# Weights, states and small tables of a one-core decoder layer, laid out by the host in reading order

## The chip, the cores and the metric

The kernel runs on one core of a Trainium2 chip. The metric is device time in microseconds (us) of one execution, given as the median of several runs. TensorE (PE) does the matrix products, VectorE (DVE) and ScalarE (ACT) the element-wise work. SyncE (SP) and GpSimd (POOL) issue the transfers (DMAs) between the chip's memory (HBM) and the on-chip buffers, SP nearly all of the loads and POOL most of the stores. All of them share 16 DMA engines.

## The reference: what is computed

One layer of a hybrid decoder, run for a prompt of 512 tokens and for 8 sampled sequences of 8 tokens, 576 tokens in all, in float32:

```python
h = rms_norm(x, norm_pre_mix)
proj = jnp.einsum('btd,de->bte', h, w_in)              # 1024 -> 8208
qkv, z, a, b, uv, gates = jnp.split(proj, SPLIT_POINTS, axis=-1)
o_a, new_buf, s_new = delta_branch(qkv, z, a, b, conv_buf, s0, ...)
o_b, v_rows = chunk_mlp_branch(uv, sgu_ln_w, sgu_ln_b, w_spatial, b_spatial)
merged = (sigmoid(g_a) * (o_a @ w_proj_a) + sigmoid(g_b) * (o_b @ w_proj_b))
x = x + rms_norm(merged @ w_out, norm_post_mix)
gate, up = jnp.split(rms_norm(x, norm_pre_ffn) @ w_ffn_in, 2, axis=-1)
x = x + rms_norm((silu(gate) * up) @ w_ffn_out, norm_post_ffn)
```

`delta_branch` is a causal convolution of width 4 over q, k and v and then a gated delta rule in chunks, which inverts a triangular matrix for each chunk and head. `chunk_mlp_branch` mixes the tokens of a chunk with a lower triangular 128 x 128 matrix for each of 8 channel groups.

## The kernel before

Activations lie with the features on the 128 partitions. A product of 1024 input features with 128 output columns is one unit: its weights are loaded as a tile `wraw` of 128 partitions x 8 x 128 floats (512 KB), ACT rounds them to a tile `whi`, DVE subtracts to get the rest `wlo`, and PE runs three products, whi with the rounded activations, wlo with the rounded activations, and whi with the rest of the activations (L255 to L307, the products at L282, a split of any other tile at L124 and L310). `wraw`, `whi` and `wlo` have two buffers each, so a load starts when the unit two before it has been split.

The program runs in stages on one in-order instruction stream for each engine: norm of x and its transposition (L192 to L252), the products u and v of the MLP branch with the chunk mixing (L313 to L562), the products with w_proj_b (L564), the delta branch in two groups of 4 heads each (L574 to L1114), the products with w_proj_a, then w_out and the norms, the FFN-in in 22 pairs (L1305), the FFN-out (L1580). In the delta branch `elim` inverts 32 x 32 blocks by a loop of small DVE instructions. It gets its input over memory (`d<-at`, `ae<-d`) and sends its result back over memory (`d<-xe`, then `XH<-d` and `XT<-d`, L796 to L812), on which the products of `combine` (L817 and on) depend. The units of the w_in products fill PE meanwhile, at fixed steps (table FILL).

A scheduler that simulates the program decides the order of each stream at build time. SP issues its DMAs in that order, and one that has to wait holds up all that follow it.

w_in is one array of 1024 rows of 8208 floats. A unit takes 128 columns of it, so a partition gets eight pieces of 512 bytes, from rows 128 apart:

```python
ld(out=raw[:, :nk], in_=w[k0 * P:(k0 + nk) * P, col:col + P].rearrange("(k p) m -> p k m", p=P))
```

w_proj_a, w_proj_b and w_ffn_in are read in the same way from rows of 1024 and 5632 floats. w_ffn_out is read in pieces of 2 KB (L1566), w_out in one run of 4 KB for each partition (L1153). Three kinds of small tables are transposed on PE after loading: the taps of the convolution (`feat`, L250), w_spatial (`wsn`, L448, and for the sampled tokens `wbn` to `wbe`, L453), and the convolution state (`scn`, whose memory has the tag `ae`, L587).

Of the kernel before, what the change touches and what calls it, by code (L numbers as in the profile page):

```python
# [28 lines left out]
CONSTS = ["ident", "mneg", "mneg_s", "seqm4", "ones", "triu", "triu_s", "ones_s", "tril_s", "seqm"]  # L29
# [3 lines left out]
def _host_consts():  # L33
# [15 lines left out]
        "tril_s": ups.T,  # L49
# [43 lines left out]
def _build(ctx, tc, I, O):  # L93
# [5 lines left out]
    w_in = I["w_in"][0]  # L99
# [1547 lines left out]
```

## Time and profile before

| | |
|---|---|
| median of 3 runs | 1226.68 us (1223.93 to 1229.81) |
| the profiled execution | 1224.94 us, of which its span is 1222.8 us |
| mean granted TensorE clock | 0.969 |
| PE busy | 1150.5 us (94%) |
| DVE, ACT, POOL busy | 717.4, 569.9, 149.7 us |
| read from HBM, written | 106.35 MB, 17.06 MB |

The span runs from the first to the last instruction. Busy is the time in which an engine worked on an instruction. PE is idle for 72 us in all. A granted clock of 1.00 is 2.4 GHz and 0.50 is 1.2 GHz; a stretch between them has had both.

### The profile page before, as it was taken

To read this page: it belongs to the slowest core of one execution; us is meant where nothing else is said; L and a number is where in the kernel's file an instruction comes from. 1 tells how busy PE (TensorE), PEld (TensorE's weight loads), DVE (VectorE), ACT (ScalarE), POOL (GpSimd) and SP (SyncE) were. 2 spreads that over 40 slices of the span, in tenths; PEclk is the share of its full clock that TensorE was granted. 3 is DMA by queue.
4 is the path that set the end of the run, shared out by engine and by line. 5 is a ranking of instruction groups with operands and counts; after the bars stand their busy time and mean duration, and the time that the engine had idled before them with its cause. 6 is when DMAs were issued, how large, how long until landed. Compare 5 with 4: busy or idle time off the path is not lost.

```text
span 1222.8 us, 20426 instructions
## 1 busy us (share of the span) xinstructions
PE 1150.5 (94%) x8144; PEld 1075.6 (88%) x8144; DVE 717.4 (59%) x1386; ACT 569.9 (47%) x1227; POOL 149.7 (12%) x230
## 2 busy tenths in 40 slices
PE   6999999999997999999998998969999999899997
PEld 5999999998996998988997886858999999888885
DVE  4329722557873456767554664667777787661323
ACT  5423323884544773558445443435445445441221
POOL 3001210002000021020010100150111111160001
PEclk9999999999997998998999999988999999999999
DMA  6911344443344354654252744023233333212222
GB/s 163 220 59 37 85 127 112 76 88 110 91 110 94 80 132 91 171 131 89 67 137 72 260 136 138 2 68 87 87 93 92 93 104 103 87 53 86 86 87 78
DMA packets 163011, 124.74 MB, mean 102 GB/s; under 512 B 14096, under 2 KB 145713, under 8 KB 162916
## 3 DMA queue, kind: packets, MB, share of 16 engines
q1 hardware_dynamic: 156226, 103.72, 32.8%
q0 software_dynamic: 6544, 19.64, 4.9%
q8 instruction: 64, 1.05, 0.3%
q14 instruction: 31, 0.25, 0.1%
q10 hardware_dynamic: 146, 0.07, 0.0%
HBM read 106.35 MB, written 17.06 MB: 101 GB/s over the span
## 4 chain that ended last, share of the span: by engine, by line
PE 52%; DMA 7%; DVE 5%; ACT 4%; issue 2%; POOL 0%; POOLq 0%; DVEq 0%; ACTq 0%; SPq 0%
PE mmps L282 13%; PE bank L1305 10%; PE mmps L1305 7%; PE bank L1580 6%; PE mmps L1580 6%; DMA wraw<-w_in 2%; PE bank L1198 2%; PE mmps L1198 1%; DVE wlo L124 1%; DMA wraw<-w_out 1%; ACT whi L256 1%; DMA wraw<-w_proj_a 1%; DMA wraw<-w_ffn_out 1%; PE bank L880 1%; DMA XH<-d 1%
## 5 line engine op out<-in xcount | busy, mean ns | idle before, releaser
L282 PE MATMUL mmps<-xh,whi 128*128 128x256 f32 (+1 forms) x896 | 273.3, 305 | 4.8 <-ACT ev L136 2.9
L282 PE MATMUL mmps<-xh,wlo 128*128 128x256 f32 (+1 forms) x896 | 271.8, 304 | 4.5 <-DVE wlo L124 4.5
L282 PE MATMUL mmps<-xl,whi 128*128 128x256 f32 (+1 forms) x896 | 271.8, 304 | 0.0
L124 DVE TENSOR_TENSOR wlo<-wraw,whi 128x1024 fp32r<-128x1024 f32 x114 | 146.6, 1287 | 208.9 <-ACT whi L256 208.7
L256 ACT CAST whi<-wraw 128x1024 fp32r<-128x1024 f32 x114 | 119.3, 1047 | 209.4 <-PE mmps L282 60.2
L282 PEld LDWEIGHTS mmps<-xh,whi 128*128 128x128 f32 x896 | 174.3, 195 | 7.5 <-ACT ev L136 4.1
L282 PEld LDWEIGHTS mmps<-xh,wlo 128*128 128x128 f32 x896 | 174.4, 195 | 6.3 <-DVE wlo L124 5.6
L282 PEld LDWEIGHTS mmps<-xl,whi 128*128 128x128 f32 x896 | 174.3, 195 | 0.7 <-issue 0.3
L127 DVE SCALAR_TENSOR_TENSOR ev<-ev,fcol 128x600 f32<-128x600 f32 x72 | 60.1, 837 | 1.8 <-ACT ev L136 0.6
L136 ACT ACT_TABLE_LOAD x40 | 51.3, 1283 | 7.6 <-DVE ans L124 3.2
L1305 PE MATMUL bank<-mh,w2hi 128*128 128x288 f32 x156 | 48.0, 308 | 5.3 <-ACT w2hi L256 5.2
L1305 PE MATMUL bank<-mh,w2lo 128*128 128x288 f32 x156 | 47.5, 305 | 2.3 <-DVE w2lo L124 2.3
L136 ACT ACTIVATE ev<-mmps 128x320 f32<-128x320 f32 (+1 forms) x73 | 30.8, 431 | 38.0 <-PE mmps L282 26.4
L1305 PE MATMUL bank<-ml,w2hi 128*128 128x288 f32 x156 | 47.3, 303 | 0.0
L1283 POOL TENSOR_TENSOR wup<-wraw,wup 128x512 f32<-128x512 f32 x20 | 26.2, 1308 | 172.5 <-DVE wup L1283 150.6
L136 ACT ACTIVATE jk<-bank 128x128 bf16<-128x128 f32 (+1 forms) x112 | 31.2, 279 | 17.6 <-PE bank L952 11.6
L282 PE MATMUL mmps<-obl,whi 128*128 128x320 f32 (+1 forms) x128 | 38.6, 303 | 0.0
L282 PE MATMUL mmps<-obh,wlo 128*128 128x320 f32 (+1 forms) x128 | 38.4, 303 | 0.0
L282 PE MATMUL mmps<-oal,whi 128*128 128x320 f32 (+1 forms) x128 | 37.5, 295 | 0.8 <-DVE oal L124 0.8
L282 PE MATMUL mmps<-oah,wlo 128*128 128x320 f32 (+1 forms) x128 | 37.6, 297 | 0.7 <-DVE wlo L124 0.7
L282 PE MATMUL mmps<-oah,whi 128*128 128x320 f32 (+1 forms) x128 | 37.1, 298 | 0.7 <-ACT oah L310 0.7
L282 PE MATMUL mmps<-obh,whi 128*128 128x320 f32 (+1 forms) x128 | 37.6, 303 | 0.0
(501 smaller groups left out, 2996.3 us busy)
## 6 DMA issues: line engine op xcount, KB each, us to landing
wraw<-w_in SPq DMA_DIRECT2D x56, 512.0 KB, 8.2
wup<-w_ffn_in SPq DMA_DIRECT2D x22, 512.0 KB, 4.6
wraw<-w_ffn_out SPq DMA_DIRECT2D x22, 512.0 KB, 3.7
wraw<-w_ffn_in SPq DMA_DIRECT2D x20, 512.0 KB, 4.0
pgd<-ev POOLq DMA_DIRECT2D x16, 288.0 KB, 5.3
ev<-pgd SPq DMA_DIRECT2D x16, 288.0 KB, 7.8
wraw<-w_proj_b SPq DMA_DIRECT2D x8, 512.0 KB, 4.5
Si<-state_delta SPq DMA_DIRECT2D x16, 256.0 KB, 4.9
```

Of the source, the lines that this page charges most:

```text
L124: return V.tensor_tensor(out=out, in0=a, in1=b, op=op)
L127: V.scalar_tensor_tensor(out=out, in0=a, scalar=s, in1=b, op0=op0, op1=op1)
L136: return S.activation(out=out, in_=a, func=f, scale=scale, accum_out=accum)
L256: a = S.copy(out=hi, in_=raw)
L282: TE.matmul(ps, lhsT=a[:, j, :], rhs=b[k][:, HF[hf]], start=(k == 0 and i == 0), stop=(k == nk - 1 and i == 2))
L880: TE.matmul(px[js, i * P:(i + 1) * P], lhsT=ZT[:, j * 160 + 32 * s:j * 160 + 32 * s + 32], rhs=Si[i, j % 2][:, s], start=(s == 0), stop=(s ...
L1198: TE.matmul(ps[q], lhsT=a[k] if t == 0 else a[k][:, o:o + P], rhs=b[k][:, q * 512:(q + 1) * 512], start=(k == 0 and i == 0), stop=(k == KT ...
L1283: (G if g else V).tensor_tensor(out=out, in0=a, in1=b, op=op)
L1305: TE.matmul(ps, lhsT=w[x][:, j], rhs=b[y][:, j], start=(first and j == 0 and i == 0), stop=(j == KH - 1 and i == 2), skip_group_check=not ...
L1580: TE.matmul(ps, lhsT=x[k] if t == 0 else x[k][:, o:o + P], rhs=unit[w][:, a_], start=(k == 0 and i == 0), stop=(k == FT - 1 and i == len(t ...
```

## The change

The host hands over other arrays. Each unit of w_in, w_proj_a, w_proj_b and w_ffn_in is one block of 128 partitions x 4 KB, in the order in which it is read, and each pair of w_ffn_out as well. The three column blocks of v, with the 16 columns of a and b behind the last, are arrays of their own (`w_v0` to `w_v2`). The states of the delta rule lie as 128 partitions x 2 KB (`state_delta_t`). The taps, w_spatial and the convolution state are transposed by the host, so the 41 transposes on PE with their copies go, and DVE multiplies w_spatial by its mask in place. Eight small loads on POOL (`wbn`) become one on SP, three loads of the convolution state on POOL become one, and the table `tril_s` is dropped from the constants. The bytes that are loaded stay the same but for that and the repeated 8 x 8 blocks. Its core:

```diff
-    w_in = I["w_in"][0]
+    def w_in(col):
+        return I["w_in_t"][col // P if col < C_AB else 32 + (col - C_U) // P if col < C_VM else 40 + (col - C_GA) // P]
...
-    feat = p0.tile([P, P], F32, name="feat", bufs=1)
-    ld(out=feat[0:96], in_=I["conv_w"][0].rearrange("t (n f) -> (t n) f", f=P))
-    ld(out=feat[96:97], in_=I["delta_norm_w"])
+    ld(out=fcol, in_=I["conv_t"])
     xh, xl = cols(XH_), cols(XL_)
-    ps = bank()
-    TE.transpose(ps[:, 0:97], feat[0:97], ident[0:97, 0:97])
-    S.copy(out=fcol, in_=ps[:, 0:97])
...
-        ld(out=raw[:, :nk], in_=w[k0 * P:(k0 + nk) * P, col:col + P].rearrange("(k p) m -> p k m", p=P))
+        ld(out=raw.rearrange("p k m -> p (k m)"), in_=w(col))
...
-            last["v"] = ld(out=raw[:, k0:k0 + 4, :e - c0],
-               in_=w_in[rows, C_VM + c0:C_VM + e].rearrange("(k p) m -> p k m", p=P))
-            if c1 > D:
-                ld(out=raw[:, k0:k0 + 4, e - c0:w], in_=w_in[rows, C_AB:C_AB + 16].rearrange("(k p) m -> p k m", p=P))
+            last["v"] = ld(out=raw[:, k0:k0 + 4].rearrange("p k m -> p (k m)"), in_=I[f"w_v{i}"][:, k0 * w:(k0 + 4) * w])
...
-        ld(out=wsn, in_=I["w_spatial"][0].rearrange("g i j -> i g j"))
+        ld(out=wst, in_=I["w_spatial_t"])
+        ld(out=wbn, in_=I["w_spatial_s"])
...
-    for s in range(8):
-        st(out=wbn[s * 8:(s + 1) * 8], in_=I["w_spatial"][0, :, 0:8, 0:8].rearrange("g i j -> i g j"))
-    wbe = wv.tile([NS, 8, NS], F32, name="wbe")
     with tc.issue_after(last["split"][1].ins):
         for g in range(8):
-            tt(wbe[:, g].rearrange("p (s j) -> p s j", j=8), wbn[:, g].unsqueeze(1).broadcast_to([NS, 8, 8]),
-               c("tril_s").rearrange("p (s j) -> p s j", j=8), ALU.mult)
-    for q in range(2):
-        ps = bank()
-        for j in range(4):
-            TE.transpose(ps[:, j * P:(j + 1) * P], wsn[:, 4 * q + j], ident)
-        tt(wst[:, 4 * q:4 * q + 4], ps.rearrange("p (a b) -> p a b", b=P),
-           c("triu").unsqueeze(1).broadcast_to([P, 4, P]), ALU.mult)
-    ps = bank()
-    for g in range(8):
-        TE.transpose(ps[:NS, g * NS:(g + 1) * NS], wbe[:, g], ident[:NS, :NS])
-    V.tensor_copy(wbt, ps[:NS].rearrange("p (a b) -> p a b", b=NS))
+            tt(wbt[:, g].rearrange("p (s i) -> p s i", i=8), wbn[:, g].unsqueeze(1).broadcast_to([NS, 8, 8]),
+               c("triu_s").rearrange("p (s i) -> p s i", i=8), ALU.mult)
+        for q in range(2):
+            tt(wst[:, 4 * q:4 * q + 4], wst[:, 4 * q:4 * q + 4], c("triu").unsqueeze(1).broadcast_to([P, 4, P]), ALU.mult)
...
-    for q in range(3):
-        scn = dt_([24, D], "ae", 1)
-        st(out=scn, in_=I["state_conv"][0].rearrange("s r f -> (s r) f")[:, q * D:(q + 1) * D])
-        ps = bank()
-        for j in range(8):
-            TE.transpose(ps[:, j * 24:(j + 1) * 24], scn[:, j * P:(j + 1) * P], ident[:24, :24])
-        V.tensor_copy(sct[:, q * 8:(q + 1) * 8, 3:], ps[:, 0:192].rearrange("p (a b) -> p a b", b=24))
+    scn = dt_([P, 24, 24], "ae", 1)
+    st(out=scn, in_=I["state_conv_t"])
+    V.tensor_copy(sct[:, :, 3:], scn)
...
-                    ld(out=Si[i, z], in_=I["state_delta"][0, 4 * z:4 * z + 4, h0 + hh].rearrange("s k v -> k s v"))
+                    ld(out=Si[i, z], in_=I["state_delta_t"][h0 + hh, z])
...
-        ld(out=raw, in_=wfi[:, col:col + P].rearrange("(k p) m -> p k m", p=P))
+        ld(out=raw.rearrange("p k m -> p (k m)"), in_=I["w_ffn_in_t"][col // P])
...
-        ld(out=raw, in_=src)
+        ld(out=raw.rearrange("p a c -> p (a c)"), in_=I["w_ffn_out_t"][q, u])
...
+    def tiles(a):
+        return a.reshape(KT, P, -1, P).transpose(2, 1, 0, 3).reshape(-1, P, KT * P)
+
+    w, out = first("w_in"), {}
+    out["w_in_t"] = tiles(np.concatenate([w[:, :C_AB], w[:, C_U:C_VM], w[:, C_GA:]], axis=1))
```

The order of the streams moves at a few places only. These are SP's rows at the start of the program, behind the five loads of x, first of before and then of the changed kernel (`dtb` holds two small vectors of the gates, `con` constants):

```order
L246 DMA feat<-conv_w 96x128
L247 DMA feat<-delta_norm_w 1x128
L261 DMA wraw<-w_in 128x8x128 x2
L466 DMA dtb<-dt_bias 128x8
L467 DMA dtb<-a_log 128x8
L261 DMA wraw<-w_in 128x8x128 x2
L358 DMA vraw<-w_in 128x4x346 x2
```

```order
L254 DMA fcol<-conv_t 128x97
L265 DMA wraw<-w_in_t 128x1024 x2
L453 DMA dtb<-dt_bias 128x8
L454 DMA dtb<-a_log 128x8
L265 DMA wraw<-w_in_t 128x1024 x2
L359 DMA vraw<-w_v 128x1384 x2
```

One small DMA ahead of the first weights is gone, and each load of weights is one run for each partition.

On PE, in the stage of w_proj_b, the first eight transposes of the convolution state stand between two units (`obh` and `obl` are the two parts of the mixed activations, `ae` the loaded state). Of before:

```order
L282 MATMUL mmps<-obh_1431,whi 128x320
L282 MATMUL mmps<-obh_1431,whi 128x256
L282 MATMUL mmps<-obh_1431,whi 128x320
L587 MATMUL bank<-ident,ae 128x24 x8
L282 MATMUL mmps<-obl_1432,whi 128x320
L282 MATMUL mmps<-obh_1431,wlo 128x320
```

And of the changed kernel:

```order
L286 MATMUL mmps<-obh_1395,whi 128x320
L286 MATMUL mmps<-obh_1395,whi 128x256
L286 MATMUL mmps<-obh_1395,whi 128x320
L286 MATMUL mmps<-obl_1396,whi 128x320
L286 MATMUL mmps<-obh_1395,wlo 128x320
```

The transposes are gone there, and nothing takes their place on PE; the other 16 of them stand in the same stage and go likewise. On DVE the copies of the state become one, which waits for the load instead of for PE. Of before and of the changed kernel:

```order
L783 MEMSET xe 72x1024
L124 TENSOR_TENSOR obl_1432<-ev,obh_1431 128x576
L124 TENSOR_TENSOR obl_1447<-ev,obh_1446 128x576
L784 MEMSET xe 72x32
L588 COPY sct<-bank 128x8x24
L124 TENSOR_TENSOR wlo<-wraw,whi 128x1024
```

```order
L766 MEMSET xe 72x1024
L133 TENSOR_TENSOR obl_1396<-ev,obh_1395 128x576
L133 TENSOR_TENSOR obl_1411<-ev,obh_1410 128x576
L767 MEMSET xe 72x32
L571 COPY sct<-ae 128x24x24
L133 TENSOR_TENSOR wlo<-wraw,whi 128x1024 x7
```

It stands at the same place, ahead of the splits of the w_proj_b units.

## Rows read from the trace of the kernel before

**Rows 1.** The page: busy us, share of the span and instructions of each engine.
```profile
PE 1150.5 (94%) x8144; PEld 1075.6 (88%) x8144; DVE 717.4 (59%) x1386; ACT 569.9 (47%) x1227; POOL 149.7 (12%) x230
```

**Rows 2.** Waits of PE, whole span: us in total, times, longest us.
```profile
PE bank L817 <- DMA XH<-d: 7.2, 1, 7.2
```

**Rows 3.** Windows: length, busy us of PE, PEld, DVE, ACT, POOL, clock, DMA share, GB/s.
```profile
155.00:160.00 5.00, 5.00 (x28) 4.99 (x28) 1.47 (x2) 1.97 (x4) 1.07 (x2) 0.66 0.08 23
285.00:290.00 5.00, 3.46 (x24) 3.01 (x23) 4.13 (x13) 0.26 (x1) 1.37 (x3) 0.92 0.13 51
290.00:295.00 5.00, 4.61 (x25) 4.09 (x24) 4.71 (x16) 1.46 (x3) 0.26 (x1) 0.74 0.72 199
365.00:380.00 15.00, 6.04 (x47) 5.34 (x46) 7.71 (x14) 5.26 (x10) 1.96 (x3) 0.82 0.79 159
380.00:395.00 15.00, 15.00 (x194) 14.76 (x193) 4.01 (x6) 7.65 (x10) 0.00 (x0) 0.61 0.23 57
475.00:480.00 5.00, 2.00 (x7) 2.00 (x8) 3.18 (x11) 1.98 (x8) 1.10 (x2) 0.69 0.36 108
480.00:485.00 5.00, 5.00 (x26) 5.00 (x26) 4.83 (x16) 0.44 (x1) 0.57 (x1) 0.62 0.36 50
500.00:505.00 5.00, 2.24 (x17) 2.04 (x16) 3.70 (x12) 3.39 (x9) 1.07 (x2) 0.92 0.54 121
505.00:510.00 5.00, 5.00 (x32) 5.00 (x32) 4.69 (x12) 2.17 (x4) 0.00 (x0) 0.73 0.84 224
...
900.00:1040.00 140.00, 140.00 (x1056) 140.00 (x1055) 109.73 (x152) 70.30 (x115) 16.81 (x13) 1.00 0.34 99
```

**Rows 4.** DMA issues, whole span: KB each, median us from issue to landing.
```profile
wraw<-w_in SPq DMA_DIRECT2D x56, 512.0 KB, 8.2
...
wraw<-w_ffn_in SPq DMA_DIRECT2D x20, 512.0 KB, 4.0
...
wraw<-w_proj_b SPq DMA_DIRECT2D x8, 512.0 KB, 4.5
...
wraw<-w_out SPq DMA_DIRECT2D x8, 512.0 KB, 4.2
```

**Rows 5.** DMA issues between 184 and 276 us alone.
```profile
wraw<-w_in SPq DMA_DIRECT2D x14, 512.0 KB, 6.9
```

**Rows 6.** Waits of ACT between 320 and 380 us.
```profile
ACT whi L256 <- DMA wraw<-w_in: 17.3, 3, 7.9
```

**Rows 7.** The chain that ended last, between 455 and 500 us: start, us, what.
```profile
462.29 12.40 DMA wraw<-w_in
...
477.97 13.18 DMA wraw<-w_in
...
493.42 7.86 DMA ev<-gcd
```

**Rows 8.** Waits of DVE between 466 and 510 us.
```profile
DVE tm L124 <- DMA ae<-d: 9.8, 1, 9.8
```

**Rows 9.** Waits of DVE between 276 and 300 us.
```profile
DVE ev L124 <- DMA ev<-pgd: 5.7, 1, 5.7
```

**Rows 10.** Timeline of PE: start, us, instructions, idle before and its releaser.
```profile
103.81 1.03 PE L448 MATMUL bank<-ident,wsn 128*128 128x128 f32 x8
104.77 0.63 PE L453 MATMUL bank<-ident,wbe 64*64 64x64 f32 x8
...
154.20 0.65 PE L587 MATMUL bank<-ident,ae 24*128 24x24 f32 x8 [2.04 <-DMA Si<-state_delta]
```

**Rows 11.** Timeline of ACT at the start.
```profile
15.28 1.04 ACT L256 CAST whi<-wraw 128x1024 fp32r<-128x1024 f32 x1 [2.94 <-DMA wraw<-w_in]
```

**Rows 12.** DMA issues 365 to 395 us: the first exchange.
```profile
XH<-d POOLq DMA_DIRECT2D x3, 64.0 KB, 7.9
```

**Rows 13.** DMA issues 510 to 600 us: the second exchange.
```profile
d<-xe POOLq DMA_DIRECT2D x1, 288.0 KB, 5.3
...
XH<-d POOLq DMA_DIRECT2D x3, 64.0 KB, 3.4
```

More of the change, by code (lines that the diff above doesn't have):

```diff
@@ L27 @@
 C_Q, C_K, C_V, C_Z, C_AB, C_U, C_VM, C_GA, C_GB = 0, 1024, 2048, 3072, 4096, 4112, 5136, 6160, 7184
-CONSTS = ["ident", "mneg", "mneg_s", "seqm4", "ones", "triu", "triu_s", "ones_s", "tril_s", "seqm"]
+CONSTS = ["ident", "mneg", "mneg_s", "seqm4", "ones", "triu", "triu_s", "ones_s", "seqm"]
 LATE = CONSTS[1:4]
@@ L48, in _host_consts @@
         "mneg_s": np.where(ups, 0.0, -1e30),
-        "tril_s": ups.T,
         "seqm4": (i[:96, None] // 8) % 4 == np.arange(4)[None, :],
@@ L68 @@
 SH = NS // 2
+CW, CH = 348, ((0, 346), (346, 694), (694, 1040))
 A_HIGH, A_LOW, LEAD = 6, 4, 4
@@ L98, in _build, with w_pa, w_pb @@
     x_p, x_s = I["x_prompt"][0], I["x_sample"].rearrange("s t d -> (s t) d")
-    w_in = I["w_in"][0]
+    def w_in(col):
+        return I["w_in_t"][col // P if col < C_AB else 32 + (col - C_U) // P if col < C_VM else 40 + (col - C_GA) // P]
+    def w_pa(col):
+        return I["w_proj_a_t"][col // P]
+    def w_pb(col):
+        return I["w_proj_b_t"][col // P]
     def pool(name, bufs, **kw):
@@ L343, in _build @@
     V.memset(ab[:, 0], 0.0)
-    NV, CW = 1040, 348
-    CH = ((0, 346), (346, 694), (694, 1040))
     pw = ExitStack()
@@ L352, in third @@
         c0, c1 = CH[i]
-        w, e = c1 - c0, min(c1, D)
-        hi, lo, raw = (wv.tile([P, KT, CW], d, name=nm, tag=nm, bufs=2)
+        w = c1 - c0
+        hi, lo, raw = (wv.tile([P, KT * CW], d, name=nm, tag=nm, bufs=2)[:, :KT * w].rearrange("p (k m) -> p k m", m=w)
                        for d, nm in ((F32R, "vh"), (F32R, "vl"), (F32, "vraw")))
         for k0 in (0, 4):
-            rows = slice(k0 * P, (k0 + 4) * P)
-            last["v"] = ld(out=raw[:, k0:k0 + 4, :e - c0],
-               in_=w_in[rows, C_VM + c0:C_VM + e].rearrange("(k p) m -> p k m", p=P))
-            if c1 > D:
-                ld(out=raw[:, k0:k0 + 4, e - c0:w], in_=w_in[rows, C_AB:C_AB + 16].rearrange("(k p) m -> p k m", p=P))
+            last["v"] = ld(out=raw[:, k0:k0 + 4].rearrange("p k m -> p (k m)"), in_=I[f"w_v{i}"][:, k0 * w:(k0 + 4) * w])
         return raw, hi, lo, w
@@ L426, in _build @@
     raw2 = third(2)
-    wsn = wv.tile([P, 8, P], F32, name="wsn")
+    wbn = wv.tile([NS, 8, 8], F32, name="wbn")
     with tc.issue_after(last["v"].ins):
-        ld(out=wsn, in_=I["w_spatial"][0].rearrange("g i j -> i g j"))
+        ld(out=wst, in_=I["w_spatial_t"])
+        ld(out=wbn, in_=I["w_spatial_s"])
         ld(out=bsp.rearrange("p g i -> p (g i)"),
@@ L568, in evac @@
             S.copy(out=sg[:, sl], in_=ps)
-        fm(I["w_proj_b"][0], m * P, obh, obl, evac)
+        fm(w_pb, m * P, obh, obl, evac)
         st(out=pgd[m], in_=sg)
@@ L1084, in pa_start @@
             act(ga, ga, AF.Sigmoid)
-            pw_[m] = wunit(I["w_proj_a"][0], m * P, 0, KT), ga, pb_
+            pw_[m] = wunit(w_pa, m * P, 0, KT), ga, pb_
         pa[m, hf] = half_ps(hf)
@@ L1257, in left @@
                     S.copy(out=hf[:, ks, TH:], in_=pv[:, :, w:])
-    wfi = I["w_ffn_in"][0]
     def raw_load(raw, col):
-        ld(out=raw, in_=wfi[:, col:col + P].rearrange("(k p) m -> p k m", p=P))
+        ld(out=raw.rearrange("p k m -> p (k m)"), in_=I["w_ffn_in_t"][col // P])
         return raw
@@ L1554, in _build @@
     wy = ctx.enter_context(pool("wy", 2))
-    wfo = I["w_ffn_out"][0]
     ytm = gt.tile([P, 5, 512], F32, name="ytm")
@@ L1565, in wpair @@
     def wpair(q, u):
-        src = wfo[2 * u * P:2 * (u + 1) * P, q * 512:(q + 1) * 512].rearrange("(a p) c -> p a c", p=P)
         wq = wy if q == 1 and NU - LAST <= u < NU - LAST + 2 else wp
@@ L1619, in _build, with _laid_out, first @@
             y_evac(q, t, pss[t])
-_INS = ["x_prompt", "x_sample", "state_delta", "state_conv", "norm_pre_mix", "w_in", "conv_w", "a_log", "dt_bias",
-        "delta_norm_w", "sgu_ln_w", "sgu_ln_b", "w_spatial", "b_spatial", "w_proj_a", "w_proj_b", "w_out",
-        "norm_post_mix", "norm_pre_ffn", "w_ffn_in", "w_ffn_out", "norm_post_ffn"]
+_INS = ["x_prompt", "x_sample", "norm_pre_mix", "a_log", "dt_bias", "sgu_ln_w", "sgu_ln_b", "b_spatial", "w_out",
+        "norm_post_mix", "norm_pre_ffn", "norm_post_ffn"]
 _OUTS = {"y_p": (1, 512, 1024), "y_s": (8, 8, 1024), "sd_p": (1, 1, 8, 128, 128), "sc_p": (1, 1, 3, 3072),
          "cv_p": (1, 1, 128, 1024), "sd_s": (1, 8, 8, 128, 128), "sc_s": (1, 8, 3, 3072), "cv_s": (1, 8, 8, 1024)}
+def _laid_out(inputs):
+    import numpy as np
+    def first(name):
+        return np.asarray(inputs[name])[0]
+    def tiles(a):
+        return a.reshape(KT, P, -1, P).transpose(2, 1, 0, 3).reshape(-1, P, KT * P)
+    w, out = first("w_in"), {}
+    out["w_in_t"] = tiles(np.concatenate([w[:, :C_AB], w[:, C_U:C_VM], w[:, C_GA:]], axis=1))
+    wv = np.concatenate([w[:, C_VM:C_GA], w[:, C_AB:C_U]], axis=1)
+    for i, (c0, c1) in enumerate(CH):
+        out[f"w_v{i}"] = wv[:, c0:c1].reshape(KT, P, c1 - c0).transpose(1, 0, 2).reshape(P, -1)
+    for name in ("w_proj_a", "w_proj_b", "w_ffn_in"):
+        out[name + "_t"] = tiles(first(name))
+    out["w_ffn_out_t"] = first("w_ffn_out").reshape(FT // 2, 2, P, 2, 512).transpose(3, 0, 2, 1, 4).reshape(2, FT // 2, P, D)
+    out["state_delta_t"] = first("state_delta").reshape(2, 4, H, P, P).transpose(2, 0, 3, 1, 4)
+    out["state_conv_t"] = first("state_conv").reshape(24, 24, P).transpose(2, 1, 0)
+    out["conv_t"] = np.concatenate([first("conv_w").reshape(96, P), first("delta_norm_w")[None]]).T
+    ws = first("w_spatial")
+    out["w_spatial_t"] = ws.transpose(2, 0, 1)
+    out["w_spatial_s"] = np.tile(ws[:, :8, :8].transpose(2, 0, 1), (8, 1, 1))
+    return out
 def kernel(**inputs):
@@ L1637 @@
         arrays[name] = np.ascontiguousarray(inputs[name])
+    for name, a in _laid_out(inputs).items():
+        arrays[name] = np.ascontiguousarray(a)
     arrays["consts"] = HOST_CONSTS
```

1 line of the change is left out of this document (removed).

## The prediction

> **What bounds the kernel now.** I read the page first, then PE's waits, then windows of the stretches in which PE stops, and last what ended each stop. The page says that PE is busy for 1150.5 of 1222.8 us [rows 1]: the kernel is bound by PE, and a shorter load is worth something only where PE stands still for it, or where the clock falls because PE stood still. From 900 to 1040 us PE is busy for 140.00 of 140 us at clock 1.00 [rows 3], so there nothing is to be had. PE's longest wait for data is 7.2 us, once, for the exchange `XH<-d` [rows 2]. The windows show five stretches of the kind sought [rows 3, 10, 11]: the start, 152 to 160, 285 to 295, 365 to 395 and 475 to 510 us. After each of the last four, PE runs on for some microseconds at a mean clock of 0.61 to 0.74. I count a stretch as its idle time plus its busy time times (1 - clock).
>
> Second, which loads are slow. A unit of w_in lands 8.2 us after its issue, one of w_proj_b 4.5, one of w_ffn_in 4.0 [rows 4]. All three bring 512 KB in 1024 pieces of 512 bytes, and only the length of the row that they are cut from differs. w_out brings the same 512 KB in 128 runs of 4 KB and lands after 4.2 [rows 4]. So short pieces alone are not slow; those of w_in are. In a stretch that holds little but the w_in products, 14 of them still take 6.9 [rows 5].
>
> **What the change does, step by step.** Every unit now has the form of w_out. I price a w_in load at 4.2 us. The bounds are 4.0 (the row of w_ffn_in) and 8.2 (no change); I take the one whose form is the same. In its quiet stretch w_in thus gains 2.7 us a load, among other traffic more.
>
> The Trainium skill, DMA: Bandwidth & Descriptors, section How a descriptor splits into AXI transactions, says that a piece which does not start on a multiple of 256 bytes costs an extra transaction. Rows of w_in are 32832 bytes long, 64 more than such a multiple, so three of four pieces need three transactions instead of two. By it I estimate at most 1.5 x 4.5 = 6.8 us for a load, and the trace has 6.9 in the quiet stretch and 8.2 over all. It agrees with the first, not with the second.
>
> A. *Transposes that go.* The 8 of w_spatial take 1.03 us, the 8 of its small blocks 0.63, the 24 of the convolution state come in three lots of 0.65 [rows 10]. PE came to the first 16 without a wait, so they are in its way: 1.03 + 0.63 + 3 x 0.65 = 3.6 us. The one of the taps (a ninth of the first price) I leave out.
>
> B. *The stop at 152 us.* PE waited 2.04 us ahead of the first eight state transposes, for the state's load [rows 10], whose row names another DMA that landed then, and then ran 5.00 us at 0.66 [rows 3], 1.70 lost. Sum 3.7. Now DVE waits there instead, in its copy, and the splits of w_proj_b are queued behind that. The load is one of 288 KB on POOL; the nearest row of that size and queue lands in 5.3 us [rows 13], and I assume (the one assumption here without a row) that it is issued where it is now. Bounds of the loss are 0 and, if it came 3 us later with nothing between, 3 us. PE has units in hand there, so I take off 0.2: 3.5.
>
> C. *The start.* ACT waits 2.94 us for the first unit of w_in before it rounds it [rows 11], and the casts of x that PE needs are queued behind. The bytes of x go first and stay the same; the two w_in units behind them, and one small load less ahead of them, come sooner. Bounds 0 and 2.94; I take 2.5, since the rest of the chain is ACT and DVE work.
>
> D. *285 to 295 us.* PE idles 1.54 + 0.39 us and loses 0.08 x 3.46 + 0.26 x 4.61 = 1.48 by the clock [rows 3], 3.4 in all. Its releaser is DVE, which had waited 5.7 us for `ev<-pgd` [rows 9], a load of SP's queue behind two of w_in. With those 2.7 us or more shorter each, that wait is nearly gone. I take 3.0; late next are DVE's own operations (4.13 and 4.71 us busy of 5).
>
> E. *365 to 395 us.* PE is busy for 6.04 of 15 us, idle 8.96, and then runs 15.00 us at 0.61, 5.85 lost [rows 3]: 14.8. Two things end here. ACT waits three times for w_in, 17.3 us, once for 7.9 [rows 6], and what it then releases (the wlo splits, the evacuations) feeds PE. Then PE waits for `XH<-d`, which lands after 7.9 us [rows 12]; the second time it takes 3.4 [rows 13], and PE does not wait for it at all. If the loads take 4.2 us, ACT's waits are gone, DVE's loop, which stands behind the same splits, ends some 4 us sooner (estimate, half of the longest of these waits), and the exchange meets an emptier queue, 7.9 - 3.4 = 4.5 us. Together 8 us against a wait of 7.2. I take 11 of 14.8: a stop of 1 to 2 us may stay, and even one of 2.04 us cost 1.70 by the clock (B).
>
> F. *475 to 510 us.* PE idles 3.00 and 2.76 us; by the clock it loses 0.31 x 2.00 + 0.38 x 5.00 + 0.08 x 2.24 + 0.27 x 5.00 = 4.1 [rows 3]: 9.8. The chain of waits has two w_in loads of 12.40 and 13.18 us and a load of 7.86 that starts after them [rows 7]. `ae<-d`, on SP behind the first, holds DVE for 9.8 us [rows 8]. Two loads of 4.2 instead of 25.6 us end both stops. I take 7.5, since DVE has the same loop to do (4.83 of 5 us busy) and may be late next.
>
> *At nothing:* the other loads. w_ffn_in would go from 4.0 to 4.2; 22 pairs of two loads at 0.2 would be 8.8 us bare, but PE does not idle there for 140 us [rows 3]. DVE's mask products and the loads that POOL no longer issues lie on engines busy for 59% and 12% [rows 1]; bare, they would cost or give some 2 us, by the price of the transposes that they replace.
>
> Sum: 3.6 + 3.5 + 2.5 + 3.0 + 11 + 7.5 = 31.1 us. The profiled execution took 1224.94 us, 1.74 less than the median: 1193.8 by it, 1195.6 by the median. I predict 1195.6.
>
> **The rivals.**
> *1. The loads do not get shorter.* Then w_in is slow because of its neighbours, not its layout, and only A and B are left: 1226.7 - 3.6 - 3.7 = 1219.4. For it speaks that 4 KB runs are no faster than 512-byte pieces (4.2 against 4.0 and 4.5 [rows 4]), and that the slowest w_in loads, of 12.40 and 13.18, have company [rows 7]; against it the 6.9 of the quiet stretch [rows 5].
> The same page of the Trainium skill, section Specifications, gives 512 bytes as the least piece for the full rate. By that rule the change gives the loads nothing, and the time is this rival's; the rows of w_ffn_in and w_out agree with it, that of w_in does not.
>
> *2. The stops move on.* The loads land early, but PE next waits for DVE, whose work at 480 us fills 4.83 of 5 us [rows 3], and a short stop drops the clock like a long one. Half of B to F: 3.6 + 34.6 / 2 = 20.9, or 1205.8. Against it: in E, DVE is busy for 7.71 of 15 us only.
>
> *3. Slower: long runs in the way of small ones.* The exchanges `d<-xe`, `XH<-d`, `ae<-d` go over the same 16 engines, in small pieces. If a run of 4 KB holds an engine so long that an exchange takes twice its time, E loses 5.3 + 7.9 = 13.2 instead of gaining [rows 12, 13] and F loses 9.8 [rows 8], while A to D keep 12.6 at full price less a little: 1226.7 - 12.6 + 13.2 + 9.8 = 1237.1. It decides where the exchanges grow by 12.6 us together. For it: only PE's first wait for `XH<-d` is on the path, and it is already 7.2. Against it: a whole load in 4 KB runs is through in 4.2 us [rows 4], so one that stands ahead of each of the two exchanges in E and of the one in F adds at most 12.6 in all, and only if none of them has cover.
>
> **How the numbers follow.** My forecast, 1186 to 1201, has 0.58; rival 2, to 1213, 0.24; rival 1, 0.10; rival 3, 0.05; still more gained, 0.03. All of each stretch would be 38.2 us, 1188.5, and smaller stops could add a few. The range is 1185 to 1212, which leaves out rivals 1 and 3 and a part of 2. A measurement of this kernel tells about 0.5% (6.1 us) from no change. Faster by over 0.5% are the forecast, rival 2 and half or more of rival 1: 0.91; within 0.5% the rest of rival 1 and the mild end of rival 3: 0.05; slower 0.04.
>
> **What would show it.** The w_in units should land in 4 to 5 us at the median (C to F right), PE should have no wait over 2 us for `XH<-d` (E), no transposes at L587 and no window at 0.66 behind them (A, B), DVE no wait of 9.8 for `ae<-d` (F). The busy time of PE should fall by 3.6 us plus what the clock gives back, some 15 us, and the mean clock rise from 0.969 to 0.98. I am wrong if the units still land in 7 or 8 us, or if they land early and PE's idle time stays near 72 us.

## The result, and the profile after

The changed kernel takes 1182.06 us at the median (1181.47 to 1182.95, 4 runs) against 1226.31 before; the ratio is 0.9636, 95% interval 0.9608 to 0.9664. It is 44 us faster, where 31.1 were forecast, and it lies 2.9 us below the low end of the range. The profiled execution took 1182.95 us, its span 1181.1.

The first row of the page of the kernel after, busy time by engine:

```profile
PE 1130.2 (96%) x8103; PEld 1058.4 (90%) x8103; DVE 719.5 (61%) x1383; ACT 572.2 (48%) x1226; POOL 154.3 (13%) x220
```

Against [rows 1] PE is busy for 20.3 us less and idle for 21.4 us less (1181.1 - 1130.2 = 50.9 against 72.3). Of the 20.3 the removed transposes are 3.6; the other 16.7 are the clock, whose mean went from 0.969 to 0.984. So each idle microsecond that went took most of another with it, as the forecast had counted.

The DMA issues of the kernel after, whole span (KB each, median us from issue to landing):

```profile
wraw<-w_in_t SPq DMA_DIRECT2D x56, 512.0 KB, 3.6
...
wraw<-w_ffn_in_t SPq DMA_DIRECT2D x20, 512.0 KB, 3.3
pgd<-ev POOLq DMA_DIRECT2D x16, 288.0 KB, 2.7
ev<-pgd SPq DMA_DIRECT2D x16, 288.0 KB, 3.9
wraw<-w_proj_b_t SPq DMA_DIRECT2D x8, 512.0 KB, 3.6
...
wraw<-w_out SPq DMA_DIRECT2D x8, 512.0 KB, 3.3
...
XH<-d POOLq DMA_DIRECT2D x6, 64.0 KB, 3.4
```

The reader is to see two things beside [rows 4]: the unit of w_in fell from 8.2 to 3.6 us, and transfers that the change did not touch fell too. The stores and loads `pgd<-ev` and `ev<-pgd` went to 2.7 and 3.9 us; on the page of before they are

```profile
pgd<-ev POOLq DMA_DIRECT2D x16, 288.0 KB, 5.3
ev<-pgd SPq DMA_DIRECT2D x16, 288.0 KB, 7.8
```

w_out, the same 4 KB runs as before, went from 4.2 to 3.3. That is not the work of w_in: in the runs below w_out takes 3.3 and 3.2 us where w_in is still slow (tables_only, w_in_old), and 3.9 and 4.5 where it is fast (w_in_only, w_in_pad_only).

Windows of the kernel after, over the stretches that answer to [rows 3] (length, busy us of PE, PEld, DVE, ACT, POOL, clock, DMA share, GB/s): the former stop at 152 us, those at 285, at 365 to 395, and at 475 to 510 (what stood at 480 us starts at 446 now).

```profile
145.00:150.00 5.00, 4.55 (x33) 4.32 (x32) 3.79 (x9) 1.35 (x2) 4.12 (x5) 1.00 0.77 257
150.00:155.00 5.00, 5.00 (x40) 4.75 (x39) 1.88 (x3) 3.29 (x6) 0.56 (x1) 1.00 0.41 135
...
275.00:280.00 5.00, 5.00 (x38) 4.55 (x37) 4.87 (x16) 1.63 (x5) 0.00 (x0) 1.00 0.75 219
280.00:285.00 5.00, 5.00 (x40) 4.62 (x41) 5.00 (x19) 3.95 (x11) 0.00 (x0) 1.00 0.01 4
...
350.00:365.00 15.00, 15.00 (x235) 14.59 (x234) 6.57 (x12) 9.03 (x14) 1.96 (x3) 1.00 0.45 118
365.00:380.00 15.00, 15.00 (x146) 14.54 (x145) 8.15 (x14) 7.25 (x14) 0.57 (x1) 1.00 0.27 91
...
440.00:445.00 5.00, 5.00 (x44) 4.96 (x43) 4.40 (x17) 2.22 (x6) 0.56 (x1) 1.00 0.66 225
445.00:450.00 5.00, 5.00 (x38) 4.95 (x38) 4.45 (x11) 1.45 (x8) 1.31 (x2) 1.00 0.51 147
...
470.00:475.00 5.00, 5.00 (x41) 5.00 (x40) 5.00 (x18) 2.22 (x11) 0.00 (x0) 1.00 0.31 105
```

PE is full at clock 1.00 in all but the first, and it stays so where DVE is busy for 4.87 or 5.00 of 5 us. Two waits of PE are all that is left between 16 and 500 us (us in total, times, longest):

```profile
PE bank L927 <- ACT w L145: 0.5, 1, 0.5
PE mmps L286 <- DVE obl L133: 0.5, 1, 0.5
```

In DVE's waits between 425 and 475 us the one for `ae<-d`, 9.8 us in [rows 8], is

```profile
DVE tm L133 <- DMA ae<-d: 1.2, 1, 1.2
```

and ACT's longest kind of wait between 300 and 360 us, which was for w_in in [rows 6], is now for PE:

```profile
ACT whi L260 <- PE mmps L286: 14.2, 7, 2.3
```

The chain that ended last, cut to 320 to 380 us, holds no DMA any more; before, it ran there through `XH<-d`:

```profile
by line: PE mmps L286 83.7%; PE bank L800 3.4%; PE bank L821 3.3%; PE bank L827 3.3%; PE bank L811 3.2%; PE bank L808 1.7%; PE bank L920 0.7%; PE bank L841 0.7%; PE bank L837 0.2%
```

To see where the time came back I set the starts of the same PE instructions in two traces against each other. Each number is how many us earlier than in the trace before an instruction starts that stood at the time on top; the runs in the other lines are those of the next section. There is one trace of each kernel. From 657 to 845 us the kernels take from 184.9 to 191.8 us for the same PE instructions (the one with slow w_ffn_in loads left out), so a difference of some us between two lines there says little.

```
time before        94    115    167    207    299    349    401    514    657    845   1210
changed kernel   2.67   4.33   9.16   9.96  14.16  14.87  29.59  39.99  40.02  40.96  41.78
w_in_pad_only    2.85   2.84   3.17   3.17   7.37   8.08  21.26  31.68  32.44  28.68  28.71
tables_only      0.55   2.19   6.99   7.78   5.82   6.47  13.52  13.44  14.07  13.38  13.61
conv_state_only  0.11   0.11   4.84   5.63   5.59   5.52   8.64   7.73   5.93   5.62   5.80
spatial_only     0.24   1.88   2.22   2.22   2.47   3.18   5.60   2.86   3.03   0.39   0.50
```

### The profile page after: what moved, and what is told of

Same layout as the page of the kernel before. It is cut to its first block, busy times and chain, and to the rows that moved or that the text cites. A ratio compares the mean times of both kernels' runs of the same rounds, so it can differ in the third digit from the quotient of the medians.

```text
span 1181.1 us, 20302 instructions
## 1 busy us (share of the span) xinstructions
PE 1130.2 (96%) x8103; PEld 1058.4 (90%) x8103; DVE 719.5 (61%) x1383; ACT 572.2 (48%) x1226; POOL 154.3 (13%) x220
## 3 DMA queue, kind: packets, MB, share of 16 engines
q8 instruction: 63, 1.03, 0.4%
## 4 chain that ended last, share of the span: by engine, by line
PE 87%; DVE 5%; ACT 3%; DMA 2%; issue 2%; SPq 0%; POOLq 0%; DVEq 0%; POOL 0%; ACTq 0%
PE mmps L286 38%; PE bank L1287 10%; PE mmps L1287 8%; PE bank L1560 6%; PE mmps L1560 6%; PE bank L389 5%; PE bank L1181 2%; PE mmps L1181 2%; DMA wraw<-w_out 1%; DVE wlo L133 1%; DMA wraw<-w_ffn_out_t 1%; PE bank L863 1%; PE bank L526 1%; DVE ev L133 1%; PE bank L733 1%
## 5 line engine op out<-in xcount | busy, mean ns | idle before, releaser
L286 PE MATMUL mmps<-xh,whi 128*128 128x256 f32 (+1 forms) x896 | 269.1, 301 | 3.1 <-ACT ev L145 2.7
L286 PE MATMUL mmps<-xl,whi 128*128 128x256 f32 (+1 forms) x896 | 267.9, 299 | 0.0
L286 PE MATMUL mmps<-xh,wlo 128*128 128x256 f32 (+1 forms) x896 | 267.3, 299 | 0.6 <-DVE wlo L133 0.6
L286 PEld LDWEIGHTS mmps<-xh,whi 128*128 128x128 f32 x896 | 170.6, 190 | 5.5 <-ACT ev L145 3.8
L286 PEld LDWEIGHTS mmps<-xh,wlo 128*128 128x128 f32 x896 | 170.6, 190 | 1.5 <-DVE wlo L133 0.9
L286 PEld LDWEIGHTS mmps<-xl,whi 128*128 128x128 f32 x896 | 170.7, 191 | 0.7 <-issue 0.3
L1265 POOL TENSOR_TENSOR wup<-wraw,wup 128x512 f32<-128x512 f32 x20 | 32.8, 1641 | 165.4 <-DVE wup L1265 89.5
L286 PE MATMUL mmps<-obl,whi 128*128 128x256 f32 (+1 forms) x128 | 37.7, 296 | 0.5 <-DVE obl L133 0.5
```

Source lines behind the costliest of these rows:

```text
L286: TE.matmul(ps, lhsT=a[:, j, :], rhs=b[k][:, HF[hf]], start=(k == 0 and i == 0), stop=(k == nk - 1 and i == 2))
L1265: (G if g else V).tensor_tensor(out=out, in0=a, in1=b, op=op)
```

## The experiments

Each run was timed against the kernel before on the same chip, whose median was between 1223.4 and 1228.2 us; a ratio is of those two. All compute the whole reference.

**Which part of the change it is.** Four kernels have one part of it or lack one.

*w_in in blocks alone*, on the kernel before:

```diff
-    w_in = I["w_in"][0]
+    def w_in(col):
+        return I["w_in_t"][...]
...
+            ld(out=raw.rearrange("p k m -> p (k m)"), in_=w(col))
```

> The kernel before with w_in (its 56 units and the three wide parts) laid out in blocks; every other table and load as before. My theory, that the stops C to F hang on the w_in loads alone: these stops and the small ones give 35.2 of the 41.7 us by which the trace after is ahead of the trace before (2.6 + 0.8 + 4.2 + 0.7 + 14.7 + 10.4 + 1.8), so 1226.3 - 35.2 = 1191, w_in loads of 3.5 to 4.2 us, and the stop at 152 us with its transposes still there. Rival, that the w_in loads became short because all other loads did too (company): w_in loads of 5 us or more and less than half of that gain, 1209 or above.

1194.5 us, ratio 0.9752 (0.9730 to 0.9774); w_in units land in 3.6 us. The gain is 30.2 us where 35.2 were expected: the theory stands, 5 us short of its number; the rival (1209 or above) falls.

*All but w_in*: the changed kernel with w_in read by its old rows.

```diff
-        ld(out=raw.rearrange("p k m -> p (k m)"), in_=w(col))
+            ld(out=raw[:, :nk], in_=w[k0 * P:(k0 + nk) * P, col:col + P].rearrange("(k p) m -> p k m", p=P))
```

> The changed kernel with w_in read as before (rows of 32832 bytes), all else new. My theory: only steps A and B are left, 4.84 + 1.66 = 6.5 us, so 1226.3 - 6.5 = 1219.8, w_in loads of 7 to 8.2 us. Rival (company): the other loads, now in runs of 4 KB, make room, w_in loads fall to 6 us or less, and 1205 or below.

1210.9 us, 0.9891 (0.9869 to 0.9912), w_in units at 8.4 us. They did not become short in better company, so the rival's ground is gone; but the gain is 13.7 us where 6.5 were expected, and that is a miss.

*Only the tables that the host transposes.*

```diff
-        ld(out=raw.rearrange("p a c -> p (a c)"), in_=I["w_ffn_out_t"][q, u])
+        ld(out=raw, in_=I["w_ffn_out"][0][2 * u * P:2 * (u + 1) * P, q * 512:(q + 1) * 512].rearrange("(a p) c -> p a c", p=P))
```

w_in, w_proj_a, w_proj_b, w_ffn_in and the delta states are read by their old rows likewise; this diff and the next are against the changed kernel, as the last one.

> Only the tables that the host transposes (taps, the spatial weights, the convolution state) are new; w_in, w_proj_a, w_proj_b, w_ffn_in, w_ffn_out and the delta states are read as before. My theory: the same 1219.8 as with w_in old and all else new, within 2 us, since the other weights' loads were hidden. Rival: the layout of the other weights has a part of its own, and this one is 5 us or more above the other.

1211.4 us, 0.9901 (0.9880 to 0.9922): the same as the run above. The layout of the other weights is worth nothing, and the tables are worth 13 us, not 6.5. The two parts multiply to 0.9752 x 0.9901 = 0.9656, inside the interval of the whole.

*The other weights old, w_in and tables new.*

```diff
+    w_pa, w_pb = I["w_proj_a"][0], I["w_proj_b"][0]
```

w_ffn_in, w_ffn_out and the delta states stand as in the run above.

> The changed kernel with w_proj_a, w_proj_b, w_ffn_in, w_ffn_out and the delta states read as before; w_in and the small tables stay new. Theory: the layout of these weights is worth nothing, 1181 to 1185. Rival: without w_in in the way they have a part of their own, 1188 or above.

1182.9 us, 0.9630 (0.9587 to 0.9673), with loads of 3.8 and 4.5 us for w_ffn_in. That is the changed kernel's time: nothing, as forecast.

**Why a w_in load was slow.** The prediction left open whether it was the 512-byte piece, the place where a piece starts, or the company. The changed kernel got its w_in units back as 1024 pieces of 512 bytes, cut from rows of a chosen length, all else new. One edit serves for all; two numbers differ.

```diff
+W_PITCH, W_OFF = 8320, 0
...
-        return I["w_in_t"][...]
+        return I["w_in_p"][:, W_OFF + u * P:W_OFF + (u + 1) * P].rearrange("(k p) m -> p k m", p=P)
...
+    out["w_in_p"] = np.zeros((D, W_PITCH), np.float32)
```

> The changed kernel with the 56 w_in units again in 1024 pieces of 512 bytes, but from rows of 33280 bytes, a multiple of 512, in place of 32832. My theory, that a w_in load was slow by where its rows begin and not by its pieces: loads of 3.6 to 4.5 us, as those of w_ffn_in were before, and 1182 to 1186. Rival (pieces): 1024 pieces against 128 is what counts in the delta part, loads of 6 us or more, 1205 or above.

> As the run with 512-byte pieces from rows of 33280 bytes (1183.0 us, loads of 4.2), but every piece starts 64 bytes later, so that none starts on a multiple of 256. Theory: where a piece starts is what costs; loads of 7 us or more and a time like that of the changed kernel with w_in read as before, 1206 to 1212. Rival: it is the odd row length itself, by which the pieces of a unit lie differently to each other, and a shift that is the same for all changes nothing: loads of 4.2, 1183.

> The same kernel with one number changed: rows of 32832 bytes again, pieces of 512, nothing shifted at the first row. Both theories expect slow loads, 7 us or more; the time should be that of w_in read as before, 1211, less up to 2.6 us, since the three wide parts of w_in stay in blocks here: 1206 to 1211. If the loads are short here, the row length is not the cause at all.

> w_in in 512-byte pieces from rows of exactly 32768 bytes. Three row lengths are known now: 32832 gives loads of 9.0 us, 33280 gives 4.2 and, shifted by 64 bytes, 3.9. Theory: a row length at or just beside 32768 sends the pieces of one load to the same places of the memory; then 32768 is as slow as 32832 or slower, 8 us or more, 1210 or above. Rival: it is the 64 bytes over a multiple of 512, by which each next row starts otherwise; then 32768 is fast, 4 us, 1183.

> w_in in 512-byte pieces from rows of 28736 bytes: 64 more than 28672, a multiple of 512 as before, but far from 32768. Theory (nearness to 32768): loads of 3.6 to 4.5 us and 1182 to 1186. Rival (the 64 bytes): loads of 7 us or more and 1206 or above. w_ffn_in from rows of 22592 bytes stayed at 3.7 to 3.9 us, which speaks for the theory, but it is another weight in another part.

> w_in in 512-byte pieces from rows of 32896 bytes, 128 over 32768. Theory of a fade (a small step from row to row beside 32768 is what costs): loads between 4.2 and 9.0 us, about 6, and a time between 1183 and 1220, which also shows where the cover of the loads ends. Theory of a pattern (only certain pairs of a large and a small step collide): fast as 33280, 4 us and 1183, or slow as 32832, nothing between.

> Rows of 33024 bytes, 256 over 32768. Fade: shorter than at 32896, about 5 us, 1183 to 1195. Pattern: 4 us and 1183, or 8 to 9 us and about 1220.

> Rows of 32704 bytes, 64 short of 32768. Theory of a step of 64 beside 32768, on whichever side: loads of 8 to 9 us and about 1220. Theory of a relation between the two terms of the sum 32768 + 64: loads of 4 us and 1183.

> Rows of 65664 bytes, twice 32832: 65536 + 128. Theory of a relation (the address bits of the large and of the small step stand the same distance apart): loads of 8 us or more, about 1220. Rival (only the neighbourhood of 32768 is slow): 4 us, 1183.

What came of them, by the median landing time of the w_in units:

```
label                row, bytes        load us   time us   ratio (95%)
w_in_512_pitch28736  28672 + 64          3.8     1183.2    0.9669 (0.9640-0.9699)
w_in_512_pitch32768  32768               4.2     1183.7    0.9665 (0.9631-0.9700)
w_in_512_pitch32896  32768 + 128         4.2     1184.5    0.9671 (0.9644-0.9699)
w_in_512_pitch33024  32768 + 256         4.3     1182.6    0.9655 (0.9632-0.9677)
w_in_512_even        32768 + 512         4.2     1183.0    0.9666 (0.9644-0.9687)
w_in_512_off64       same, shifted 64    3.9     1183.5    0.9632 (0.9587-0.9676)
w_in_512_pitch32704  32768 - 64          7.5     1205.8    0.9851 (0.9815-0.9886)
w_in_512_pitch65664  65536 + 128         8.5     1216.1    0.9929 (0.9904-0.9953)
w_in_512_pitch64     32768 + 64          9.0     1220.3    0.9933 (0.9913-0.9953)
```

The rows of the DMA issues for two of these kernels, which differ in one number; first rows of 33280 bytes, then of 32832:

```profile
wraw<-w_in_p SPq DMA_DIRECT2D x56, 512.0 KB, 4.2
```

```profile
wraw<-w_in_p SPq DMA_DIRECT2D x56, 512.0 KB, 9.0
```

Same pieces, same number of them, same neighbours in the program: only the length of the row is left, with the size and place of the array that go with it. (Where the array lies in memory was not varied by itself; rows of 32832 bytes were slow in every kernel here that reads a weight from them.) The piece falls as a cause (nothing is lost by 1024 of them at 33280), and so does the place where a piece starts (off64). My own theories fell in part as well: nearness to 32768 (32768 itself and 32896 are fast), a fade (nothing lies between), 64 bytes over a multiple of 512 (28736 is fast). Of the theory of a relation between the two terms, the doubled row bears out the main point, 65536 + 128 is slow, but it wanted 32704 fast, and that takes 7.5 us. What all three slow lengths have is a power of two with a 512th of it added or taken off; none of the six fast settings has that. This was seen after the runs, on three lengths, and no run was made to test it. Why such a row length makes a load slow stays open.

The time of w_in_512_pitch64 is a miss of its own: 1206 to 1211 were expected and 1220.3 came. Against w_in_old, whose row length is the same and whose loads take 8.4 us, it gained 7.9 us in place of 13.7. So the landing time of the loads does not set the time of the kernel by itself. By the starts the two differ most from 349 to 401 us and from 401 to 514; what makes the difference is open.

The last run of this kind leaves the kernel before as it was, and only fills up its rows:

```diff
+    arrays["w_in"] = np.pad(arrays["w_in"], ((0, 0), (0, 0), (0, 112)))
```

> The kernel before, word for word, with each row of w_in filled up by the host from 32832 to 33280 bytes. Theory of the row length: w_in loads of about 4.2 us and the 30 us that w_in in blocks gave by itself: 1193 to 1197. Rival (the blocks have a part of their own, in the loads of the wide parts at the start above all): 1198 or above.

1194.6 us, 0.9741 (0.9718 to 0.9764), that is, the whole of what the blocks of w_in gave by themselves (0.9752). The row of its DMA issues, with the kernel's old code and old pieces, against the 8.2 of [rows 4]:

```profile
wraw<-w_in SPq DMA_DIRECT2D x56, 512.0 KB, 4.1
```

**What a slow load costs where there is cover.** The prediction put w_ffn_in at nothing. These two give it pieces from rows of 22592 and of 32832 bytes.

```diff
-        ld(out=raw.rearrange("p k m -> p (k m)"), in_=I["w_ffn_in_t"][col // P])
+        ld(out=raw, in_=I["w_ffn_in_p"][:, col:col + P].rearrange("(k p) m -> p k m", p=P))
...
+    out["w_ffn_in_p"] = np.zeros((D, 5648), np.float32)
```

> The changed kernel with w_ffn_in in 512-byte pieces from rows of 22592 bytes, 64 more than a multiple of 512 (before, it was 22528, a multiple). If the row length makes a load slow whatever the weight is, its 44 loads go from 3.3 and 3.7 us to about 7 or 8. What that costs: my theory, that only the delta part has no cover for it: 1182 to 1187. Rival, that slow loads cost wherever they are: some 4 us for each of 22 pairs, of which a part shows, 1200 or above. If its loads stay at 4 us, the slowness belongs to w_in's place and not to its rows.

1184.0 us, 0.9628 (0.9577 to 0.9680): the loads stayed at 3.7 and 3.9 us, and so did the time.

> The changed kernel with w_ffn_in in 512-byte pieces from rows of 32832 bytes, the row length that made w_in slow (with 22592 its loads stayed at 3.7 and 3.9 us and the time at 1184.0). Theory of the row length: its 44 loads now take 7 us or more. What they cost: theory of cover, that PE works through without a stop and the loads are issued far ahead: 1182 to 1190. Rival, that a slow load costs in the feed-forward part too, at least 1 us for each of 22 pairs: 1205 or above.

1276.9 us, 1.0431 (1.0398 to 1.0463): the rival, and by far. From its DMA issues, its windows, and the waits of ACT between 760 and 1100 us:

```profile
wup<-w_ffn_in_p SPq DMA_DIRECT2D x22, 512.0 KB, 9.8
...
wraw<-w_ffn_in_p SPq DMA_DIRECT2D x20, 512.0 KB, 8.1
```

```profile
900.00:920.00 20.00, 15.06 (x104) 14.49 (x103) 10.71 (x16) 6.98 (x12) 2.56 (x2) 0.90 0.48 74
```

```profile
ACT whi L260 <- DMA wraw<-w_ffn_in_p: 108.3, 18, 11.1
```

Inside the stretch that [rows 3] show as full for 140 us, PE now idles a quarter of the time and the clock is 0.90. The instructions that stand at 787.28 and 999.39 us in the changed kernel stand at 794.94 and 1095.74 here: 300.8 us in place of 212.1. The cover that hides a load of 4 us does not hide one of 8 to 10; and the slowness goes with the row, whatever weight it is.

**The small tables taken apart.** Why did they give 13 us, and not 7?

```diff
+    scn = dt_([P, 24, 24], "ae", 1)
+    st(out=scn, in_=I["state_conv_t"])
+    V.tensor_copy(sct[:, :, 3:], scn)
-    for q in range(3):
...
```

> The kernel before with only the convolution state transposed by the host (one load and one copy in place of 3 loads, 24 transposes and 3 copies). The small tables together gave 13.2 us, 7.8 of them up to 206 us, where I had forecast 7.1 for A and B, and 7.0 more around 370 us, less 2.3 lost at 290. Theory: the convolution state gives the stop at 152 us alone, 4.8 us, and with it the shift in the delta part, 10 to 13 in all, so 1212 to 1215. Rival: the shift around 370 us comes from the spatial tables or the order of loads, and this edit gives 4 to 6: 1219 to 1221.

1219.05 us, 0.9964 (0.9946 to 0.9981): 4.4 us, the rival's number.

The other half keeps these lines as before and takes the spatial tables and the taps from the host:

```diff
+        ld(out=wst, in_=I["w_spatial_t"])
+        ld(out=wbn, in_=I["w_spatial_s"])
-        ld(out=wsn, in_=I["w_spatial"][0].rearrange("g i j -> i g j"))
...
```

> Only the spatial tables and the taps come from the host; the convolution state is transposed on PE, all weights are read as before. By the forecast of step A it gives the two rows of transposes, 1.7 us: 1223 to 1224. If the parts of the tables add up to the 13.2 of all of them, it gives 13.2 - 4.4 = 8.8: about 1216. If neither alone shifts the delta part as both do, it gives 1 to 4.

1223.8 us, 0.9978 (0.9962 to 0.9993): 2.8 us. By themselves the two give 4.35 + 2.79 = 7.1, what the forecast had for A and B; together 13. The table of starts shows the place: up to 207 us both together have 7.78, what the halves have (5.63 + 2.22 = 7.85). At 401 us the sums still agree (8.64 + 5.60 = 14.24 against 13.52). Then the halves lose in the stops that are still there, of the delta part and of the stretch up to 845 us (conv_state_only is 8.64 ahead at 401 us and 5.62 at 845, spatial_only 5.60 and 0.39), and both together lose little of what they win. What sets that is open. It is no fixed worth of the tables: in w_in_512_pitch64, where they are new and w_in is slow as well, 7.9 us are gained in all.

## Why the prediction was wrong

Right: the loads of w_in became short, the stops C to F went with them, nothing took their place, and no other weight's layout counted. Wrong: the size, by 10.7 us of the trace (41.8 against 31.1).

- **A and B**, 7.1 forecast. The starts give 1.66 from 94 to 115 us (priced 1.03 + 0.63) and 4.83 from 115 to 167 (1.95 + 3.5): 6.5. Right. DVE waits 2.3 us for the new load of the state, which lands after 6.2 us, not 5.3, and PE still idles 0.45 us in the window from 145.
- **C**, 2.5: measured 2.67.
- **D**, 3.0 of 3.4: measured 4.2. **E**, 11 of 14.8: measured 14.7. **F**, 7.5 of 9.8: measured 10.4.

Here is the step that failed. In E I wrote "a stop of 1 to 2 us may stay", in F "DVE has the same loop to do (4.83 of 5 us busy) and may be late next", and for these took 3.8, 2.3 and 0.4 us off stretches that in truth came back whole, D and F with a little more from beside the windows. D, E and F together measured 29.3 where I took 21.5. That is 7.8 of the 10.7. (The sum in E is also short by the rule that I set for it: the first of its windows loses 0.18 x 6.04 = 1.1 us by the clock, so the whole stretch is 15.9 and all of them together 39.3.)

In D and F a full window of DVE was taken for a sign that PE would wait for DVE next. It is none here. In the stretch of F, with the wait for `ae<-d` at 1.2 us, DVE is busy for 4.40, 4.45 and 5.00 of 5 us, and PE does not wait for it. In the trace of before a window without any work of DVE stood ahead of the full one at 480 us:

```profile
470.00:475.00 5.00, 4.96 (x41) 4.66 (x39) 0.00 (x0) 1.16 (x4) 0.00 (x0) 1.00 0.60 160
```

So what filled it was at least in part work that the wait for `ae<-d` [rows 8] had held up; how much, no run shows.

In E a term was missing, the store `d<-xe` that goes ahead of `XH<-d`. Of before and of the changed kernel, in the first exchange:

```profile
d<-xe POOLq DMA_DIRECT2D x1, 288.0 KB, 7.3
```

```profile
d<-xe POOLq DMA_DIRECT2D x1, 288.0 KB, 4.1
XH<-d POOLq DMA_DIRECT2D x3, 64.0 KB, 3.9
```

The store is issued at 363.48 us before and at 345.40 now, 18.1 earlier, of which PE had gained 14.9 up to there: so DVE's loop ended 3.2 us sooner (4 estimated), the store took 3.2 less (nothing estimated), and `XH<-d` 4.0 less (4.5 estimated). That is 10.4 us, not 8. It was needed: two short waits of PE just ahead, 1.4 us for ACT and 0.4 for DVE, went as well, by the starts PE came to `XH<-d` 2.3 us sooner, and 7.2 + 2.3 = 9.5 had to be made up. By the 8 us of the forecast 1.5 would have stayed, as it said; with the store 0.9 was to spare. A run bears this out: in w_in_only `XH<-d` took 5.0 us instead of 3.9, and PE waited for it again, for 0.3. That E came back whole hung on less than 1 us, which is partly luck.

- **Stops that I did not list**: 0.8 us between 167 and 207, 0.7 between 299 and 349, 1.8 after 514. That is 3.3 more. The sum left them out, and the low end, 1185, allowed 3.5 for them below 1188.5, which with D and F above their ceilings was not enough. The remaining -0.4 is A, B and C.
- **The price of a load**, 4.2: measured 3.6. Its bound of 4.0 from w_ffn_in was no bound for runs of 4 KB, since that row was read in pieces of 512 bytes: it is 3.3 in the changed kernel, but still 3.8 in rest_old, where w_in is fast and its own layout is the old one. This cost nothing, as the table of row lengths shows: from 3.6 to 4.3 us a load the time is 1182.1 to 1184.5. Between 4.3 and 7.5 there is no run, so where the cover of a load ends is open; above, the time is not set by the load alone (1210.9 at 8.4 us in w_in_old, 1216.1 at 8.5 in w_in_512_pitch65664).
- **What makes the load slow.** The prediction gave it to "the length of the row that they are cut from", and that held. Its estimate beside it did not: the Trainium skill, DMA: Bandwidth & Descriptors, section How a descriptor splits into AXI transactions, lets a piece cost an extra transaction where it does not start on a multiple of 256 bytes. In w_in_512_off64 every piece starts 64 bytes past one, and the load takes 3.9 us, against 4.2 without the shift. If the rule acts here, it costs nothing that these runs can tell. The Trainium skill, on that page, section Specifications, names 512 bytes as enough for the full rate; the 3.8 to 4.3 us of 512-byte pieces against the 3.6 of 4 KB runs nearly agree. The Trainium skill, on that page, section Latency and other measured facts, reports copies that slow down at row lengths of 2, 4 and 8 MiB, and recover at 4 MiB by 4 KiB of filling but not by 192 bytes. No run here has rows as long. At 32768 bytes the power of two itself is fast, 64 more is slow, 128 more is fast, which that section does not cover.
- **The rivals.** 1 (the loads do not get shorter) and 2 (the stops move on to DVE, 1205.8) fall with the windows above. 3 (long runs in the way of small exchanges) is reversed: `XH<-d` in the first exchange went from 7.9 [rows 12] to 3.9 us, and all 288 KB exchanges through `pgd` to half.
- **At nothing**: rest_old shows it for the loads. But the reason, that PE does not idle there, holds for the lengths of before alone: at 8 to 10 us the same 44 loads cost some 95 us.

By the runs, not by the places in one trace, w_in gave 32.0 (w_in_pad_only) against 24.0 forecast for C to F, and the tables 13.2 (tables_only) against 7.1 for A and B. The first is the failed step above. The second is the 6 us that the tables gave beyond their forecast: they come around 370 us while w_in is slow, and after 657 us where it is not (w_in_pad_only loses 3.8 between 657 and 845, the changed kernel loses nothing). The windows between these two instructions, of before, of w_in_pad_only and of the changed kernel, show what kind of time the latter is:

```profile
657.00:845.00 188.00, 163.73 (x943) 143.07 (x943) 118.48 (x208) 87.69 (x170) 28.88 (x31) 0.93 0.38 116
624.53:816.35 191.82, 167.71 (x945) 146.43 (x944) 118.89 (x208) 87.95 (x170) 28.97 (x31) 0.90 0.37 113
616.95:804.06 187.11, 162.39 (x944) 141.67 (x943) 118.61 (x208) 87.80 (x170) 28.94 (x31) 0.94 0.34 116
```

PE idles for 24.3, 24.1 and 24.7 us there; what differs is its busy time and the granted clock. So this part came by the clock and not by a stop that the tables ended; what moves the clock there is not shown. The part around 370 us is stop E, shorter with slow loads too: in tables_only PE waits 4.8 us for `XH<-d`, not 7.2, behind a store that lands after 4.8 us, not 7.3. Why the store is faster there is open.

## What to carry to other kernels

When a load is slow among others of the same size and pieces, first look at the length of the row that it is cut from, and try another: 448 bytes of filling in each row, with no line of the kernel changed, gave 32 of the 44 us. Price a stop by every transfer in the chain that ends it, the store as well as the load behind it, and do not take a busy engine for a late one: a window full of its work that stands behind a wait of that engine says little about the time when the wait is gone. And a load that is hidden is hidden up to a length: look for the length at which the cover ends before calling a transfer free.

## What the runs showed of the hardware

Rows of 32768 + 64, 32768 - 64 and 65536 + 128 bytes make a 512 KB load in 512-byte pieces take 9.0, 7.5 and 8.5 us; rows of 32768, 32896, 33024, 33280 and 28736 bytes take 3.8 to 4.3. w_ffn_in, which was fast from rows of 22592 bytes (3.7 and 3.9 us), takes 8.1 and 9.8 from rows of 32832. Slow loads also slow some of their company: with w_in's rows filled up, and nothing else changed, `ev<-pgd` lands after 4.4 us in place of 7.8, and `XH<-d` in the first exchange after 3.3 in place of 7.9. Not all of it goes with w_in: in w_in_512_pitch64, with loads of w_in at 9.0 us, `XH<-d` takes 7.5 there, but `ev<-pgd` 4.6. Between the same two instructions, at 657 and 845 us of the trace before, the mean granted clock was 0.90 in w_in_pad_only and 0.94 in the changed kernel, though PE idled for the same 24 to 25 us.
